# Slot ids loaded one expert block earlier, narrow blocks turned two steps later, and second-norm statistics split between two engines

## The chip, the cores and the metric

One Trainium2 chip, of which the kernel uses one core. The metric is the device time of one execution in microseconds (us); every kernel is run several times and the median is quoted. The engines of the core are PE (TensorE, matrix products), ACT (ScalarE), DVE (VectorE), POOL (GpSimd) and SP (SyncE, which here only issues transfers). Each takes its instructions in program order, and transfers (DMAs) run beside them.

## The reference, cut to what matters

The model is one layer: a token mixer (two recurrent head groups), a first layer norm, a mixture of 32 experts, a second layer norm. There are 2048 tokens of width 1024, all in float32. The change touches the last two parts.

```python
# experts: every token goes to 2 of 32 experts
hid = jax.nn.silu(xb @ w1[e]) * (xb @ w3[e])      # 1024 -> 512
y = hid @ w2[e]                                   # 512 -> 1024
f[tok] += weight * y
# second norm
r = ALPHA * h + g2 * f
mu, var = mean(r), mean((r - mu) ** 2)
out = (r - mu) * rsqrt(var + 1e-6) * ln2_g + ln2_b
```

## The kernel before, in words

Before the experts, each token's normed row is written to a DRAM tensor `u2D`, `ALPHA * h` to a DRAM accumulator `accD`, and a table `idxD` in DRAM receives, for each expert, the token number and the weight of each of its rows ("slot ids": 8 bytes a row). The experts are ranked by their load, and `ROWS` says how many rows are computed for the expert of each rank (288 down to 80). What exceeds it is left to a loop over further blocks of 128 rows at the end.

**Blocks.** The expert stage is a list of 33 blocks, unrolled. Block 0 is 128 rows of the largest expert. From block 1 on, wide blocks (odd numbers up to 27; 288-128 = 160, 224, 176, 160 or 144 rows, class `Wide`) and narrow blocks (even numbers; 80 to 128 rows, class `Block`) alternate; blocks 28 to 32 are all narrow, of 128 rows. For a block, the rows are gathered from `u2D` by an indirect DMA on POOL's queue into a tile `X` (three buffers; a wide block takes two), which needs the block's ids in a small tile `ix` (loaded by SP from `idxD`). PE transposes `X` four chunks at a time (L1330, "turn"), and ACT and DVE split the transposed chunk into a high and a low part (L1334, L1335) since the products are made of three reduced-precision products each. Then come four steps (`up(0)` to `up(3)`) of products with w1 and w3, the gate (`hidden`), a transpose of the gated rows for a narrow block (`turn_hidden`), and the products with w2 (`down`, L1341 to L1343). `put` weights the result on DVE (L1350) and adds it into `accD` by an indirect DMA on POOL's queue (L1351).

**Weights.** An expert has 12 pieces of 512 KB. SP fetches them into eight `raw` buffers (L1307); ACT casts the high part (L1314), DVE subtracts for the low part (L1315). `pump` does the next split that buffers allow, and SP's next fetch stands right behind it in SP's queue.

**Order.** Everything is written out by the loop over blocks `t` and steps `s_`. At step 0 of block t, `prepare(t + 2)` loads the ids of block t+2 on SP and issues its gather on POOL at once. A wide block t+1 is turned in all four steps of block t. A narrow block t+1 is turned in its steps 0 and 2. The downs of a narrow block t-1 are emitted in step 1 of block t, those of a wide block in its own step 3 and the next block's step 3.

**Second norm.** At the end, `accD` is read back as 16 tiles `f` of 128 tokens. Four functions, one tile apart, run over them: `stats2` (mean and variance: two `bn_stats` and one `bn_aggr` on DVE), `scale2` (`rstd_of`: an add of epsilon on DVE, L901, and a power on POOL, L902), `norm2` (the bias -mean*rstd as a one-column DVE instruction, L1665, and the normalization on ACT, L1666), and `affine2` (times the gain on DVE, L1669, where the gain lies in PSUM; plus the bias on POOL, L1673, or on DVE for the tiles in `DADD`, L1671; then the store). `ASTAT` lists tiles whose statistics would be taken by two passes on ACT; before, it is empty.

Of the kernel before, what the change touches and what calls it, by code (L numbers as in the profile page):

```python
# [10 lines left out]
I32 = mybir.dt.int32  # L11
# [3 lines left out]
ALU = mybir.AluOpType  # L15
# [12 lines left out]
ALPHA = 2.0 ** 0.25  # L28
EPS = 1e-6
FAR = -3.0e38  # L30
ASTAT = ()
DADD = (13, 14, 15)
LAG = 1

ROWS = [288] + [224] * 4 + [176] * 3 + [160] * 2 + [144] * 4 + [128] * 6 + [112] * 2 + [96] + [80] * 9
# [39 lines left out]
def hymba_kernel(ctx, tc, xT, ctxT, x, small, rows, ada_w, w_in, gate_w, w_out, router_w, w1, w3, w2, out):  # L75
    nc = tc.nc
    dve, act, pe, pool, sp = nc.vector, nc.scalar, nc.tensor, nc.gpsimd, nc.sync
# [604 lines left out]
    slots = []  # L682
# [62 lines left out]
    for si in range(len(slots), 3, -1):  # L745
        a, b, c, d = slots[si - 4:si]
        turn = si == len(slots) or slots[si][0] != d[0] or (si - 4 > 0 and slots[si - 5][0] != a[0])
# [157 lines left out]
    with ExitStack() as st:  # L905
# [239 lines left out]

        def turn_lead(X):
            pts = []
# [140 lines left out]
    with ExitStack() as st:  # L1288
# [5 lines left out]
        ex = st.enter_context(tc.tile_pool(name="ex", bufs=2))  # L1294
# [21 lines left out]
            k = 4 if n < 8 else 2  # L1316
            return [t.rearrange("p (k c) -> p k c", k=k) for t in (hi, lo)]

        def gather(row, n):

            ix = ex.tile([128, 2], I32, name="ix", tag="ix", bufs=8)
            sp.dma_start(ix[:n], idxD[bass.ds(row, n), :])
            X = ex.tile([128, D], F32, name="X", tag="X", bufs=3)
            pool.indirect_dma_start(out=X[:n], out_offset=None, in_=u2D, in_offset=bass.IndirectOffsetOnAxis(ap=ix[:n, 0:1], axis=0))  # L1324
            return ix, X

        def turned(X, n, k0):
            pt = psT.tile([128, 4, 128], F32, name="ptx", tag="pt")
            for k in range(4):
                pe.transpose(pt[:, k, :n], X[:n, 128 * (k0 + k):128 * (k0 + k) + 128], ident[:n, :n])  # L1330
            return pt[:, :, :n]

        def split_rows(xh, xl, pt):
            act.copy(xh, pt)  # L1334
            dve.tensor_sub(xl, pt, xh.bitcast(F32))  # L1335
# [9 lines left out]
        def put(py, ix, n):  # L1345

            y = ex.tile([128, D], F32, name="y", tag="y")
            for nh in range(2):
                s = slice(512 * nh, 512 * nh + 512)
                dve.scalar_tensor_tensor(y[:n, s], py[nh][:n], ix[:n, 1:2].bitcast(F32), g2[:n, s], op0=ALU.mult, op1=ALU.mult)  # L1350
            pool.indirect_dma_start(out=accD, out_offset=bass.IndirectOffsetOnAxis(ap=ix[:n, 0:1], axis=0), in_=y[:n], in_offset=None, compute_op=ALU.add)  # L1351
# [4 lines left out]
        class Block:  # L1356
# [3 lines left out]
            def __init__(self, row, n, weights, slot):  # L1360
                self.row, self.n, self.w, self.slot = row, n, weights, slot

            def gather(self):
                self.ix, self.X = gather(self.row, self.n)

            def places(self):
                x = ex.tile([128, KC, 2, 128], F32R, name="xx", tag=self.slot, bufs=1)
# [11 lines left out]
            def turn(self, i):  # L1379
                if i == 0:  # L1380
                    self.places()
                k0 = 4 * i
                split_rows(self.xh[:, k0:k0 + 4, :], self.xl[:, k0:k0 + 4, :], turned(self.X, self.n, k0))
# [37 lines left out]
        class Wide:  # L1421
# [5 lines left out]
            def __init__(self, row, n, weights, slot):  # L1427
                self.row, self.n, self.m, self.w, self.slot = row, n, n // 2, weights, slot

            def gather(self):  # L1430
                self.src = [gather(self.row + self.m * a, self.m) for a in range(2)]

            def turn(self, i):
                n, m = self.n, self.m
                if i == 0:
                    self.x = ex.tile([128, KC, 2, n], F32R, name="xw", tag=self.slot, bufs=1)
                a, k0 = i // 2, 4 * (i % 2)
                s = slice(m * a, m * a + m)
                split_rows(self.x[:, k0:k0 + 4, 0, s], self.x[:, k0:k0 + 4, 1, s], turned(self.src[a][1], m, k0))

            def up(self, s, kk):

# [29 lines left out]
                down(self.hh[:, k, s], self.hl[:, k, s], self.w[8 + k], k, self.py, self.m)  # L1472

            def put(self, part):
                put(self.py, self.src[part][0], self.m)

        SP = (mybir.EngineType.SP,)
        SPP = (mybir.EngineType.SP, mybir.EngineType.Pool)
# [17 lines left out]
        nb = len(blocks)  # L1496
        wide = [n > 128 for _, _, n, _ in blocks] + [False]

        def reg(s_):
            if s_ not in regs:  # L1500
                regs[s_] = nc.values_load(etab[0:1, sched[s_]:sched[s_] + 1], engines=SP, min_val=0, max_val=31)
            return regs[s_]
# [27 lines left out]
        if True:  # L1530
            B = []
            rest = overflow()

            def prepare(t):
                if t < nb:
                    s_, o, n, _ = blocks[t]
                    slot = "xw" if wide[t] or (not wide[t - 1] and B[t - 1].slot == "xs") else "xs"
                    B.append((Wide if wide[t] else Block)(reg(s_) * LE + o, n, weights[s_], slot))
                    B[t].gather()

            def finish(t, part):
                for k in range(4):
                    while 8 + k not in B[t].w:
                        pump(1)
                    B[t].down(k, part)
                    if blocks[t][3] and part == B[t].parts - 1:
                        state["down"] += 1
                    pump(1)
                B[t].put(part)

            def turn(t, i):
                if t < nb and i < B[t].turns:
                    B[t].turn(i)

            def used(t, i):
                if blocks[t][3]:
                    state["up"] += 2

            def late(t):
                if t == nb // 2:  # L1560
                    sp.dma_start(l2b, rows[0:1, 4096 + 3 * D:4096 + 4 * D].to_broadcast([128, D]))


            fetch_to(2)
            B.append(Block(reg(0) * LE, 128, weights[0], "xs"))
            prepare(1)
            prepare(2)
            fetch_to(NRAW)
            B[0].lead(lead_ix, lead_pt)
            pump(4)  # L1570
            for t in range(nb):
                for s_ in range(4):
                    while 2 * s_ + 1 not in B[t].w:
                        pump(1)
                    if wide[t]:
                        for kk in range(4):
                            B[t].up(s_, kk)
                            if kk == 1:
                                pump(1)
                    else:  # L1580
                        B[t].up(s_)
                    used(t, s_)
                    if s_ % 2 and wide[t]:
                        B[t].hidden(s_ // 2)
                    if s_ == 3 and not wide[t]:
                        B[t].hidden()
                    if s_ == 0 and t and not wide[t - 1]:
                        B[t - 1].turn_hidden()
                    if t + 1 < nb and wide[t + 1]:
                        turn(t + 1, s_)  # L1590
                    elif s_ % 2 == 0:
                        turn(t + 1, s_ // 2)
                    pump(2)
                    if s_ == 0:
                        if t:
                            prepare(t + 2)
                        late(t)
                    if s_ == 2 and t:
                        next(rest, 0)
                    if s_ == 1 and t and not wide[t - 1]:  # L1600
                        finish(t - 1, 0)
                    if s_ == 3 and t and wide[t - 1]:
                        finish(t - 1, 1)
                    if s_ == 3 and wide[t]:
                        finish(t, 0)
            B[nb - 1].turn_hidden()
            finish(nb - 1, 0)
# [4 lines left out]
        with tc.For_i(0, nov) as i:  # L1612
            oe = ex.tile([1, 2], I32, name="oe", tag="oe")
            for k in range(2):
                sp.dma_start(oe[:, k:k + 1], otD[0:1, bass.ds(i + k * (NOV + 2), 1)])
            e = nc.values_load(oe[0:1, 0:1], engines=ENG, min_val=0, max_val=31)
            row = nc.values_load(oe[0:1, 1:2], engines=ENG, min_val=0, max_val=32 * LE - 128)
            b = Block(row, 128, {}, "xs")
            b.gather()
            b.turn(0)  # L1620
            b.turn(1)
            for n in range(12):
                b.w[n] = split(fetch(e, n), n)
            for s_ in range(4):
                b.up(s_)
            b.hidden()
            b.turn_hidden()
            for k in range(4):
                b.down(k)
            b.put()  # L1630


    with ExitStack() as st:
# [12 lines left out]
        mv, rs = {}, {}  # L1646

        def stats2(i):

            mv[i] = gs.tile([128, 2], F32, name="mv2")  # L1650
            if i in ASTAT:
                sq = gp.tile([128, D], F32, name="sq2", bufs=1)
# [9 lines left out]
            rs[i] = rstd_of(gs, mv[i][:, 1:2], 1, 1.0 / D if i in ASTAT else 1.0)  # L1662

        def norm2(i):
            dve.scalar_tensor_tensor(mv[i][:, 0:1], mv[i][:, 0:1], 1.0 if i in ASTAT else -1.0, rs[i], op0=ALU.mult, op1=ALU.mult)  # L1665
            act.activation(f[i], f[i], AF.Identity, scale=rs[i], bias=mv[i][:, 0:1])  # L1666

        def affine2(i):
# [60 lines left out]
```

## Time and profile before

| | |
|---|---|
| median of 3 runs | 2242.07 us (2241.68 to 2252.21) |
| profiled execution, its own time | 2243.1 us |
| its span, first to last instruction | 2241.0 us |
| mean granted clock of PE in it | 0.957 |
| first `up` of the experts, last `put` | 1353.8 us, 2167.1 us |
| second norm, first `bn_stats` to the last instruction | 2178.0 us to 2237.4 us |

Times in the profile count from the first instruction of the span. A row of the timeline says when an instruction or a merged run of them started, how long it took, and in brackets how long its engine had stood idle and for what. "xN" is the number of instructions merged.

### The profile page before, as it was taken

To read this page: it belongs to the slowest core of one execution; us is meant where nothing else is said; L and a number is where in the kernel's file an instruction comes from. 1 tells how busy PE (TensorE), PEld (TensorE's weight loads), DVE (VectorE), ACT (ScalarE), POOL (GpSimd) and SP (SyncE) were. 2 spreads that over 40 slices of the span, in tenths; PEclk is the share of its full clock that TensorE was granted. 3 is DMA by queue.
4 is the path that set the end of the run, shared out by engine and by line. 5 is a ranking of instruction groups with operands and counts; after the bars stand their busy time and mean duration, and the time that the engine had idled before them with its cause. 6 is when DMAs were issued, how large, how long until landed. Compare 5 with 4: busy or idle time off the path is not lost. (4 is left out here: it accounts for less than half of the span.)

```text
span 2241.0 us, 34527 instructions
## 1 busy us (share of the span) xinstructions
PE 2048.3 (91%) x12440; PEld 1810.6 (81%) x12440; DVE 1713.6 (76%) x2632; ACT 1167.9 (52%) x1863; POOL 700.3 (31%) x532
## 2 busy tenths in 40 slices
PE   7999998999998999989799987999999999999960
PEld 3788778999997988889588877888888888788850
DVE  6677776866866888888677875788877788787869
ACT  3456554644655545535444324566665666565633
POOL 5121142222333232231466661112222223222116
PEclk9999999999999999999899987999999999999985
DMA  8324333323334144244765527899998989898965
GB/s 267 107 102 138 105 127 129 131 94 123 105 100 153 58 162 145 70 149 165 263 206 174 158 78 277 245 294 303 294 303 276 306 295 299 286 310 301 334 215 237
DMA packets 180515, 441.56 MB, mean 197 GB/s; under 512 B 27365, under 2 KB 69349, under 8 KB 179830
## 3 DMA queue, kind: packets, MB, share of 16 engines
q1 hardware_dynamic: 155446, 385.18, 49.6%
q0 software_dynamic: 15088, 46.81, 8.5%
q10 hardware_dynamic: 9808, 7.34, 1.0%
q8 instruction: 99, 1.62, 0.3%
q14 instruction: 74, 0.61, 0.1%
HBM read 358.63 MB, written 80.63 MB: 196 GB/s over the span
## 5 line engine op out<-in xcount | busy, mean ns | idle before, releaser
L1315 DVE TENSOR_TENSOR wlo<-raw,whi 128x1024 fp32r<-128x1024 f32 x384 | 452.3, 1220 | 55.4 <-ACT whi L1314 51.0
L356 PE MATMUL pp<-uh,wh 128*128 128x384 f32 (+2 forms) x1248 | 445.5, 357 | 4.6 <-ACT uh L246 2.3
L357 PE MATMUL pp<-ul,wh 128*128 128x384 f32 (+2 forms) x1248 | 429.1, 344 | 4.8 <-DVE ul L247 4.6
L358 PE MATMUL pp<-uh,wl 128*128 128x384 f32 (+2 forms) x1248 | 427.6, 343 | 3.0 <-DVE wl L247 3.0
L1314 ACT CAST whi<-raw 128x1024 fp32r<-128x1024 f32 x384 | 382.5, 1050 | 38.8 <-PE pye L1342 23.1
L1452 PE MATMUL ph<-xw,whi 128*128 128x448 f32 (+3 forms) x896 | 259.6, 365 | 1.6 <-DVE hid L1403 1.6
L356 PEld LDWEIGHTS pp<-uh,wh 128*128 128x128 f32 x1248 | 238.5, 191 | 26.3 <-ACT rgs L614 5.9
L357 PEld LDWEIGHTS pp<-ul,wh 128*128 128x128 f32 x1248 | 238.4, 191 | 19.8 <-DVE ul L247 10.3
L358 PEld LDWEIGHTS pp<-uh,wl 128*128 128x128 f32 x1248 | 237.5, 190 | 13.4 <-DVE wl L247 4.6
L1453 PE MATMUL ph<-xw,wlo 128*128 128x224 f32 (+3 forms) x896 | 222.3, 248 | 0.0
L388 POOL TENSOR_SCALAR mraw<-mraw,sil 128x512 f32<-128x512 f32 x56 | 99.7, 1780 | 363.1 <-DMA mraw<-in_ada_w_dram 363.1
L1351 POOL DMA_INDIRECT accD<-y,ix x46 | 113.1, 2459 | 316.5 <-DVE y L1350 315.9
L1452 PEld LDWEIGHTS ph<-xw,whi 128*128 128x128 f32 x896 | 174.7, 195 | 7.2 <-DVE hid L1403 1.8
L1395 PE MATMUL ph<-whi,xx 128*80 128x256 f32 (+3 forms) x608 | 175.3, 288 | 3.7 <-ACT whi L1314 3.5
L1453 PEld LDWEIGHTS ph<-xw,wlo 128*128 128x128 f32 x896 | 177.2, 198 | 1.2
L1397 PE MATMUL ph<-wlo,xx 128*80 128x256 f32 (+3 forms) x608 | 172.2, 283 | 1.4 <-DVE wlo L1315 1.4
L1396 PE MATMUL ph<-whi,xx 128*80 128x256 f32 (+3 forms) x608 | 171.6, 282 | 0.0
L1324 POOL DMA_INDIRECT X<-u2D,ix x46 | 65.5, 1425 | 320.8 <-PE pye L1343 134.3
L489 PE MATMUL pa<-Q,km 128*128 128x128 f32 x896 | 124.0, 288 | 19.2 <-DVE Q L492 11.9
L489 PEld LDWEIGHTS pa<-Q,km 128*128 128x128 f32 x896 | 118.4, 193 | 25.1 <-ACT K L419 7.0
L247 DVE TENSOR_TENSOR wl<-wr,wh 128x1024 fp32r<-128x1024 f32 x84 | 109.7, 1306 | 34.8 <-ACT wh L246 34.7
L490 DVE COPY_PREDICATED A<-masks,pa 128x384 f32<-128x384 uint8 (+1 forms) x140 | 84.1, 618 | 46.9 <-PE pa L489 44.1
(350 smaller groups left out, 4566.7 us busy)
## 6 DMA issues: line engine op xcount, KB each, us to landing
raw<-in_w_dram SPq DMA_DIRECT2D x384, 512.0 KB
wr<-in_w_in_dram SPq DMA_DIRECT2D x84, 512.0 KB
mraw<-in_ada_w_dram SPq DMA_DIRECT2D x64, 256.0 KB
aw<-in_ada_w_dram SPq DMA_DIRECT2D x16, 512.0 KB
fx<-in_x_dram SPq DMA_DIRECT2D x16, 512.0 KB
accD<-fr SPq DMA_DIRECT2D x16, 512.0 KB
u2D<-fu SPq DMA_DIRECT2D x16, 512.0 KB
f<-accD SPq DMA_DIRECT2D x16, 512.0 KB
```

Source lines behind the costliest of these rows:

```text
L356: pe.matmul(ps, wh[:, k, :], uh[:, k, :], start=k == 0, stop=False)
L357: pe.matmul(ps, wh[:, k, :], ul[:, k, :], start=False, stop=False)
L358: pe.matmul(ps, wl[:, k, :], uh[:, k, :], start=False, stop=k == KC - 1)
L489: pe.matmul(pa[:, c, :], km[:, s:s + 128], cut(Q, s, [(2 * b, 64 // b), (T + b, 2), (1, b)]), start=True, stop=True)
L1314: act.copy(hi, raw)
L1315: dve.tensor_sub(lo, raw, hi.bitcast(F32))
L1351: pool.indirect_dma_start(out=accD, out_offset=bass.IndirectOffsetOnAxis(ap=ix[:n, 0:1], axis=0), in_=y[:n], in_offset=None, compute_op=AL ...
L1395: pe.matmul(p, self.xh[:, k, :], wh[:, kk, :], start=k + g == 0, stop=False, skip_group_check=True)
L1396: pe.matmul(p, self.xl[:, k, :], wh[:, kk, :], start=False, stop=False, skip_group_check=True)
L1397: pe.matmul(p, self.xh[:, k, :], wl[:, kk, :], start=False, stop=k == KC - 1, skip_group_check=True)
L1452: pe.matmul(p[:, :2 * n], wh[:, kk, f], self.x[:, k].rearrange("p h t -> p (h t)"), start=k == 0, stop=False)
L1453: pe.matmul(p[:, :n], wl[:, kk, f], self.x[:, k, 0, :], start=False, stop=k == KC - 1)
```

## The change

Three things change. First, the load of a block's ids (`slots`) is separated from its gather. At step 0 of block t the kernel now gathers block t+2, whose ids were loaded during block t-1, and loads the ids of block t+3; the id tile has nine buffers instead of eight. Second, a narrow block t+1 is turned in steps 2 and 3 of block t instead of 0 and 2. Third, in the second norm the tiles 1, 3, 5, 7, 9, 11 and 13 take their statistics on ACT (a pass `Identity` with scale -1/1024 and a sum, then a pass `Square` with that sum as bias, summed again), the bias is added on DVE for tiles 3, 7, 11 and 15 instead of 13, 14 and 15, and the one-column instruction of `norm2` becomes a `tensor_scalar` whose operand `rs` is a per-partition scalar, where it was a `scalar_tensor_tensor` with `rs` as a second tensor.

```diff
-ASTAT = ()
-DADD = (13, 14, 15)
+ASTAT = (1, 3, 5, 7, 9, 11, 13)
+DADD = (3, 7, 11, 15)
...
-        def gather(row, n):
-
-            ix = ex.tile([128, 2], I32, name="ix", tag="ix", bufs=8)
+        def slots_of(row, n):
+
+            ix = ex.tile([128, 2], I32, name="ix", tag="ix", bufs=9)
             sp.dma_start(ix[:n], idxD[bass.ds(row, n), :])
+            return ix
+
+        def gather(ix, n):
+
             X = ex.tile([128, D], F32, name="X", tag="X", bufs=3)
             pool.indirect_dma_start(out=X[:n], out_offset=None, in_=u2D, in_offset=bass.IndirectOffsetOnAxis(ap=ix[:n, 0:1], axis=0))
-            return ix, X
+            return X
...
             def prepare(t):
+
                 if t < nb:
+                    B[t].gather()
+                place(t + 1)
+
+            def place(t):
+                if len(B) <= t < nb:
                     s_, o, n, _ = blocks[t]
                     slot = "xw" if wide[t] or (not wide[t - 1] and B[t - 1].slot == "xs") else "xs"
                     B.append((Wide if wide[t] else Block)(reg(s_) * LE + o, n, weights[s_], slot))
-                    B[t].gather()
+                    B[t].slots()
...
             B.append(Block(reg(0) * LE, 128, weights[0], "xs"))
+            place(1)
+            place(2)
             prepare(1)
             prepare(2)
             fetch_to(NRAW)
...
                     if t + 1 < nb and wide[t + 1]:
                         turn(t + 1, s_)
-                    elif s_ % 2 == 0:
-                        turn(t + 1, s_ // 2)
+                    elif s_ >= 2:
+                        turn(t + 1, s_ - 2)
...
         def norm2(i):
-            dve.scalar_tensor_tensor(mv[i][:, 0:1], mv[i][:, 0:1], 1.0 if i in ASTAT else -1.0, rs[i], op0=ALU.mult, op1=ALU.mult)
+            dve.tensor_scalar(mv[i][:, 0:1], mv[i][:, 0:1], rs[i], 1.0 if i in ASTAT else -1.0, op0=ALU.mult, op1=ALU.mult)
             act.activation(f[i], f[i], AF.Identity, scale=rs[i], bias=mv[i][:, 0:1])
```

## Rows read from the trace of the kernel before

**Rows 1.** Busy time of engines by stretch: start:end, length, engines, clock, DMA share, GB/s.

```profile
1500.00:1600.00 100.00, 99.54 (x643) 87.04 (x642) 80.06 (x93) 62.39 (x80) 22.54 (x13) 1.00 0.91 296
...
2180.00:2241.00 61.00, 0.00 (x0) 0.00 (x0) 56.25 (x96) 19.85 (x16) 39.70 (x29) 0.50 0.62 251
```

**Rows 2.** Waits, 1390 to 2165 us: us in total, times, longest.

```profile
PE ptx L1330 <- DMA X<-u2D,ix: 19.3, 9, 4.4
```

**Rows 3.** Timeline of PE: transposes at step 0 of wide blocks 13, 25, 27, 29.

```profile
1684.20 0.44 PE L1330 MATMUL ptx<-ident,hid 80*128 80x80 f32 x4
...
1985.72 0.55 PE L1330 MATMUL ptx<-ident,hid 112*128 112x112 f32 x4
...
2032.66 0.60 PE L1330 MATMUL ptx<-ident,hid 128*128 128x128 f32 x4
2037.69 1.09 PE L1330 MATMUL ptx<-ident,X 128*128 128x128 f32 x4 [4.42 <-DMA X<-u2D,ix]
...
2084.71 0.60 PE L1330 MATMUL ptx<-ident,hid 128*128 128x128 f32 x4
```

**Rows 4.** Busy time by stretch, right behind a wait of PE.

```profile
1690.00:1700.00 10.00, 10.00 (x48) 8.21 (x48) 6.61 (x9) 5.74 (x9) 2.12 (x2) 0.81 0.65 183
```

**Rows 5.** Timeline of POOL and of SP's queue in block 12.

```profile
1667.28 3.87 POOL L1351 DMA_INDIRECT accD<-y,ix  x1 [11.34 <-DVE y L1350]
1671.40 0.34 SPq L1322 DMA_DIRECT2D ix<-idxD  x1
1679.88 1.69 POOL L1324 DMA_INDIRECT X<-u2D,ix  x1 [8.74 <-PE pye L1342]
```

**Rows 6.** Busy time by stretch: two blocks without a wait; a late narrow block.

```profile
1985.70:2032.70 47.00, 46.44 (x327) 40.39 (x327) 39.23 (x47) 30.25 (x40) 13.65 (x6) 1.00 0.94 313
...
2096.30:2116.30 20.00, 18.89 (x138) 17.72 (x137) 18.27 (x20) 13.83 (x16) 2.77 (x3) 1.00 1.03 383
```

**Rows 7.** Timeline at the start of the experts: SP's queue, ACT.

```profile
1354.23 2.03 SPq L1322 DMA_DIRECT2D ix<-idxD  x3
...
1360.21 1.04 ACT L1314 CAST whi<-raw 128x1024 fp32r<-128x1024 f32 x1 [5.25 <-DMA raw<-in_w_dram]
```

**Rows 8.** Timeline of the second norm, one period of it.

```profile
2189.29 2.34 POOL L1673 TENSOR_TENSOR f<-f,l2b 128x1024 f32<-128x1024 f32 x1 [0.72 <-DVE f L1669]
...
2190.59 1.06 DVE L1665 SCALAR_TENSOR_TENSOR mv<-mv,rstd 128x1 f32<-128x1 f32 x1
2191.57 1.21 DVE L1669 TENSOR_TENSOR f<-f,l2g 128x1024 f32<-128x1024 f32 x1
2191.59 0.55 POOL L902 TENSOR_TENSOR rstd<-rstd,nhalf 128x1 f32<-128x1 f32 x1
...
2192.70 1.27 DVE L1658 BATCH_NORM_STATS2 bs<-f 128x6 f32<-128x512 f32 x2
```

**Rows 9.** Timeline of the second norm: its first gain product, and its end.

```profile
2184.43 1.22 DVE L1669 TENSOR_TENSOR f<-f,l2g 128x1024 f32<-128x1024 f32 x1
...
2228.64 1.22 DVE L1669 TENSOR_TENSOR f<-f,l2g 128x1024 f32<-128x1024 f32 x1
2229.89 2.08 DVE L1671 TENSOR_TENSOR f<-f,l2b 128x1024 f32<-128x1024 f32 x1
2230.85 1.53 POOL L902 TENSOR_TENSOR rstd<-rstd,nhalf 128x1 f32<-128x1 f32 x1
...
2236.13 1.23 DVE L1671 TENSOR_TENSOR f<-f,l2b 128x1024 f32<-128x1024 f32 x1
```

**Rows 10.** Timeline of the first norm: DVE beside a POOL product.

```profile
1207.89 3.45 POOL L1029 TENSOR_TENSOR fr<-fr,l1g 128x1024 f32<-128x1024 f32 x1 [3.83 <-DVE fu L1027]
...
1209.42 0.21 DVE L1101 TENSOR_SCALAR tok<-tok,c 128x1 f32<-128x1 f32 x1
```

**Rows 11.** Instructions of ACT by line: duration ns min/median/max.

```profile
L969 ACT ACTIVATION_READ_ACCUMULATOR sq<-fo x64: 185/187/190, 1076.4 to 1291.7; 128x1 f32 x64
...
L1666 ACT ACTIVATE f<-f,mv,rstd x16: 1239/1241/1242, 2183.0 to 2232.6; 128x1024 f32<-128x1024 f32 x16
```

More of the change, by code (lines that the diff above doesn't have):

```diff
@@ L1361, in __init__, with slots @@
                 self.row, self.n, self.w, self.slot = row, n, weights, slot
+            def slots(self):
+                self.ix = slots_of(self.row, self.n)
             def gather(self):
-                self.ix, self.X = gather(self.row, self.n)
+                self.X = gather(self.ix, self.n)
             def places(self):
@@ L1428, in __init__, with slots @@
                 self.row, self.n, self.m, self.w, self.slot = row, n, n // 2, weights, slot
+            def slots(self):
+                self.ix = [slots_of(self.row + self.m * a, self.m) for a in range(2)]
             def gather(self):
-                self.src = [gather(self.row + self.m * a, self.m) for a in range(2)]
+                self.X = [gather(ix, self.m) for ix in self.ix]
             def turn(self, i):
@@ L1438, in turn @@
                 s = slice(m * a, m * a + m)
-                split_rows(self.x[:, k0:k0 + 4, 0, s], self.x[:, k0:k0 + 4, 1, s], turned(self.src[a][1], m, k0))
+                split_rows(self.x[:, k0:k0 + 4, 0, s], self.x[:, k0:k0 + 4, 1, s], turned(self.X[a], m, k0))
             def up(self, s, kk):
@@ L1474, in put @@
             def put(self, part):
-                put(self.py, self.src[part][0], self.m)
+                put(self.py, self.ix[part], self.m)
         SP = (mybir.EngineType.SP,)
@@ L1618, in hymba_kernel @@
             b = Block(row, 128, {}, "xs")
+            b.slots()
             b.gather()
```

## The prediction, made before any run of the change

> **What bounds the kernel now.** I read the busy times by stretch first. In the expert stage PE is the bound: 99.5 us of 100 at full clock in its first half, with DVE at 80, ACT at 62 and the DMA engines at a share of 0.91 [rows 1]. In the second norm PE does nothing and DVE is busy 56 of 61 us. The rest of the kernel, up to 1340 us, isn't touched by the diff. So two questions decide: where does PE stand still among the experts, and what paces the second norm?
>
> The waits answer the first. PE stands 19.3 us in nine waits, all of them transposes of gathered rows that have not landed [rows 2]. I then looked up each on PE's timeline: none lies before 1684 us; seven, together 16.9 us, stand at step 0 of wide blocks 13 to 27, where the rows of the next, narrow block are turned, and the last two, 2.5 us, in the closing run of narrow blocks. The reader should see one of them in [rows 3]: the gated rows are transposed at 2032.66, the next four transposes only at 2037.69.
>
> A wait costs more than its length. Just behind one, PE is busy for 10 us of 10 but was granted a clock of 0.81, part of the time 1.2 instead of 2.4 GHz [rows 4]. So I priced the waits by whole periods instead. From block 13 to block 29 there are eight pairs of a wide and a narrow block, 2084.71 - 1684.20 = 400.5 us; the pair without a wait takes 2032.66 - 1985.72 = 46.9 us [rows 3]. Eight pairs at 47 are 376 us: the waits with their clock cost 24 us.
>
> POOL's timeline and SP's queue tell why the rows are late [rows 5]. In block 12 POOL is through with its previous scatter at 1667.28 + 3.87 = 1671.15. SP issues the id load for block 14 only at 1671.40, because it stands behind weight fetches that wait for buffers. The gather starts at 1679.88, after 8.74 us idle. (The profile puts that idle time down to a product of PE; that is an inference from semaphores, and the id load in flight explains it.) PE asks for these rows right after 1684.20 + 0.44 and gets them at 1687.5, so issue to landing is 7.6 us.
>
> **The expert stage, part by part.** With ids a block early nothing holds the gather but the scatter ahead of it on POOL: it goes at about 1671.3 instead of 1679.9 and lands at about 1679, before step 0 needs it. The turn moves as well: a wide block takes about 27 us (a pair's 47 less the 20.0 of a narrow block [rows 6]), steps 0 and 1 about half of that, so rows are asked for near 1696. The margin is some 17 us; all seven waits should go. I take -24 us (bounds: -16.9, the waits alone, if the clock stays; -24.5).
>
> The last two waits, 2.5 us, lie where PE isn't alone: in a late narrow block DVE is busy 18.3 of 20.0 us and the DMA share is 1.03 at 383 GB/s, against 0.94 at 313 GB/s in the clean pair [rows 6]. With the transfers full, weights will take over part of the wait. Between 0 and -2.5 I take -1.
>
> What the moved steps cost: the splits of a turn (on ACT and DVE) now come one or two steps before the product that reads them instead of three or four. Behind a wide block 24 downs stand between, so this is 0. Among the four last narrow blocks the cover is one `up`, under 3 us, and DVE is nearly full; bounds 0 to +4, I take 0, since ACT has 6 us in 20 idle there [rows 6]. The 46 id loads and 46 gathers stay as many. The ninth id buffer keeps SP free: block t+3's ids overwrite those of block t-3, whose last scatter is issued at the end of block t-2, with a whole wide block, 27 us, between.
>
> At the start the new order loads ids of blocks 1, 2 and 3 instead of 1 and 2 before the third weight piece: five SP loads instead of three, which took 2.03 us, or 0.68 each [rows 7]. ACT stands 5.25 us for that piece, so nothing covers it: +1.4 us (bounds 0 and +1.4).
>
> **The second norm, part by part.** Its period is 3.57 us a tile, (2191.57 - 2184.43) / 2 [rows 8, 9]. The rows show a ring, and DVE's work isn't what fills it: POOL's bias add ends at 2191.63; the one-column DVE instruction, which needs only the power finished long before, runs from 2190.59 to 2191.65 and ends with that add, then the gain product follows (1.13 us to the next instruction), and only then POOL's next add. So a two-tensor DVE instruction in SBUF stands until POOL is through. The bias add on DVE does the same (2.08 us at 2229.89 against 1.23 at 2236.13), and POOL's power behind it stands too (1.53 against 0.55); a gain product with its second operand in PSUM runs 1.22 at 2228.64 regardless.
>
> Does the new `tensor_scalar` also stand? In the first norm such an instruction, one column with a pointer scalar, took 0.21 us in the midst of a POOL product from 1207.89 to 1211.34 [rows 10]. So I price it at 0.21 (bounds 0.21 and the 1.06 of the old one), and the ring is cut. What then paces is the busiest engine over four tiles (two with ACT statistics, one DVE add, three POOL adds):
> - the SBUF path that POOL and two-tensor DVE instructions take in turn: 3 x 2.35 + 4 x 0.55 + 1.2 = 10.4 us;
> - ACT: four normalizations at 1.24, and two tiles with two more passes, each 1.24 + 0.19 for reading its sum [rows 11]: 5.0 + 5.7 = 10.7 us. Passes of this length with a sum aren't in the trace; the normalization row is the nearest;
> - DVE: two tiles of statistics at 1.27, four gain products at 1.13, the add at 1.2 and a dozen one-column instructions at 0.21 or less: under 10.8 us.
>
> All three lie close, 10.7 against 14.3 before: 2.68 a tile. From the first gain product, sixteen tiles take 42.8 us and the last bias add 1.2, 44 us, where before it was 2236.13 + 1.23 - 2184.43 = 52.9 [rows 9]. Queues that take turns in order lose a little of such a sum, about 1 us: -8 us (bounds -3 and -11).
>
> The Trainium skill speaks against this step. "SBUF — State Buffer", section "Who interferes with whom", says that VectorE and GpSimd share one port pair as an exclusive lock, that a two-input SBUF instruction takes part in it, and that `tensor_scalar` can too when it enters a two-port mode. By that the one-column instruction might stand as before; the row of 0.21 us says it doesn't, and the measurement decides.
>
> **The sum**, against the profiled execution's own 2243.1 us: -24 - 1 + 1.4 - 8 = -31.6, so 2211.5. The median of the runs stands 1.0 below that execution: 2210.
>
> **The rivals.**
> - *The transfers take back half.* DMA is busy 0.94 in the clean pair, and 1.03 is what a full stretch shows [rows 6]; PE's waits were also time for weights to catch up (a share of 0.65 behind one [rows 4]). Against it: the clean pair ran its 46.9 us at 0.94. If half the 24 comes back as waits for weights: 2222. Chance 0.12.
> - *The one-column instruction still stands* behind POOL. Then the ring stays; only the statistics move, which weren't its limit, and only the end changes: about -3 instead of -8, so 2215. Chance 0.08, for the skill's rule and because the exact operands aren't in the trace.
> - *The rows still come late*, because POOL's scatter, not the ids, holds the gather. Then only the second norm gains and the start loses: 2235.5. Against it stand 8.74 us of idle POOL. Chance 0.04.
> - *Slower: ids held too long.* If SP stood at an id load for its buffer, the weight fetches behind it would stand as well. Eight raw buffers at one piece per 2 us (a pair's 24 pieces in 47 us) cover 16 us, and the buffer is free 27 us before, so the scatter would have to release it some 43 us later than I think before PE notices; from there each of 30 blocks pays. At 1.5 us a block more, it eats the gain of 32 and 13 beyond: 2255. Chance 0.02.
> - *More than forecast*: the waits' clock is worth more and the second norm reaches its -11: 2204. Chance 0.06.
>
> The forecast itself has 0.68. The range 2199 to 2225 holds it and all but the third and fourth rivals. A difference of 0.5%, 11 us, is about what a measurement of this kernel can tell from none. Faster by more: 0.94; within: 0.04; slower: 0.02.
>
> **What would show it.** Right: no wait of PE for `X`; POOL's gathers directly behind scatters; granted clock 1.00 from 1400 us to the end of the experts; pairs of 47 us up to block 28; weights at the start 1.4 us later; in the second norm one-column instructions of 0.2 us, a period near 2.7 and ACT the busiest. Wrong: PE waiting for casts of weights with the DMA share at 1.03, one-column instructions of 1 us, or id loads waiting for scatters on SP.

## The result, and the profile after

| | before | after |
|---|---|---|
| median of the runs, us | 2247.14 (4 runs, 2241.68 to 2253.80) | 2209.06 (4 runs, 2205.26 to 2214.66) |
| profiled execution, us | 2243.1 | 2208.83 |
| its span, us | 2241.0 | 2206.8 |
| mean granted clock | 0.957 | 0.963 |

The ratio of the times on record is 0.985, with a 95% interval of 0.9819 to 0.9881: 1.2 to 1.8% faster. (The medians of the table alone divide to 0.983; the one of the kernel before was 2242.07 ahead of the forecast, and a fourth run, 2253.80, moved it.) The forecast was 2210, with a range of 2199 to 2225.

Because totals move by several microseconds from one execution to the next, I compare stages. The marks are the first `up` product of the experts, the transposes of `hid` at step 0 of a block, and the first statistics of the second norm; all are read from PE's and DVE's timelines.

| stage, us | before | after | difference |
|---|---|---|---|
| start to the first `up` (not touched) | 1353.8 | 1355.0 | +1.15 |
| first `up` to step 0 of block 1 | 31.09 | 31.65 | +0.56 |
| to block 13 | 299.28 | 299.25 | 0.0 |
| block 13 to block 29, eight pairs | 400.51 | 372.17 | -28.3 |
| block 29 to the last `hid` | 73.76 | 71.58 | -2.2 |
| to the first statistics of the second norm | 19.53 | 20.87 | +1.3 |
| to the end of the program | 63.0 | 56.3 | -6.7 |

They add up to -34.2, the difference of the spans; the forecast's sum was -31.6.

First, the waits of PE among the experts, new kernel (total us, times, longest), to set beside [rows 2]:

```profile
PE ptx L1334 <- DVE hid L1410: 1.4, 1, 1.4
PE ph L1462 <- DVE hid L1410: 1.3, 1, 1.3
PE pye L1345 <- ACT hw L1338: 1.0, 1, 1.0
```

These are the three largest that are left from 1380 us on. No wait for `X` is among the rest either: 19.3 us in nine waits are gone. What that is worth shows in PE's busy time and clock over the whole stretch of the eight pairs, before and then after:

```profile
1684.20:2084.71 400.51, 381.52 (x2579) 331.26 (x2578) 313.69 (x366) 240.80 (x317) 101.16 (x47) 0.97 0.90 295
```

```profile
1685.88:2058.05 372.17, 370.87 (x2579) 322.53 (x2577) 312.30 (x365) 239.48 (x317) 105.05 (x47) 1.00 0.98 317
```

The columns are those of [rows 1]. PE's idle time fell from 19.0 to 1.3 us, which gives 17.7 of the 28.3 us, and its busy time by 10.65, while the granted clock rose from 0.97 to 1.00. Next, POOL and SP's queue in block 12, to set beside [rows 5], and PE's timeline in blocks 13 and 29, to set beside [rows 3]:

```profile
1668.97 3.87 POOL L1355 DMA_INDIRECT accD<-y,ix  x1 [13.96 <-DVE y L1354]
1672.57 0.93 SPq L1322 DMA_DIRECT2D ix<-idxD  x2
1673.15 0.95 POOL L1328 DMA_INDIRECT X<-u2D,ix  x1 [0.31 <-PE ptx L1334]
```

```profile
1685.88 0.44 PE L1334 MATMUL ptx<-ident,hid 80*128 80x80 f32 x4
...
1700.30 0.44 PE L1334 MATMUL ptx<-ident,X 80*128 80x80 f32 x4
...
2058.05 0.60 PE L1334 MATMUL ptx<-ident,hid 128*128 128x128 f32 x4
```

The gather starts 0.31 us behind the scatter instead of 8.74 us, and every gather from 1644 to 2060 us starts 0.30 or 0.31 us behind POOL's instruction ahead of it. The ids that SP loads just then are those of a later block. PE turns the gathered rows at 1700.30, 14.4 us after step 0 begins and 27 us after the gather was issued. Between the first and the last mark lie the eight pairs: 372.17 us, 46.5 each.

The busy time by stretch, in the columns of [rows 1], shows the transfers' side: the middle of the pairs, a late narrow block, and 4 us among the last downs.

```profile
1830.00:1880.00 50.00, 49.94 (x347) 42.99 (x347) 42.52 (x52) 31.90 (x44) 15.34 (x8) 1.00 0.98 310
2097.00:2117.00 20.00, 20.00 (x147) 18.91 (x147) 19.86 (x21) 15.78 (x19) 1.56 (x1) 1.00 1.03 376
2130.00:2134.00 4.00, 3.32 (x10) 2.16 (x9) 0.69 (x1) 0.58 (x1) 0.00 (x0) 0.60 0.56 109
```

PE is busy 49.94 of 50 us at full clock with the DMA share at 0.98; PE's list has no wait for weights there. In the late narrow block PE now has 20.0 of 20.0 us and DVE 19.86 ([rows 6] had 18.89 and 18.27). The last row belongs to the +1.3 us that the forecast didn't have: a granted clock of 0.60 while the last downs run, so 1.2 GHz for most of these 4 us. The kernel before had 1.00 at this place.

The start, to set beside [rows 7]: the first `up` of PE, SP's id loads, PE's first transposes of block 1's rows, ACT's cast of the third weight piece.

```profile
1354.98 0.55 PE L1402 MATMUL ph<-whi,xx 128*128 128x256 f32 x1 [3.43 <-ACT whi L1314]
...
1355.39 3.68 SPq L1322 DMA_DIRECT2D ix<-idxD  x5
...
1362.36 0.79 PE L1334 MATMUL ptx<-ident,X 80*128 80x80 f32 x4 [0.51 <-DMA X<-u2D,ix]
...
1364.05 1.04 ACT L1314 CAST whi<-raw 128x1024 fp32r<-128x1024 f32 x1 [7.94 <-DMA raw<-in_w_dram]
```

Five loads take 3.68 us on the queue, and the third piece is cast 9.07 us behind the first `up`, where before it was 6.38 (1360.21 - 1353.83). In the same stretch the kernel before had a wait for rows that [rows 2], which begins at 1390 us, doesn't count:

```profile
1363.31 0.80 PE L1330 MATMUL ptx<-ident,X 80*128 80x80 f32 x4 [3.20 <-DMA X<-u2D,ix]
```

It is 0.51 us in the new kernel.

Last, one stretch of the second norm, to set beside [rows 8], and the one-column line over all sixteen tiles (duration in ns: min/median/max):

```profile
2172.50 2.36 POOL L1692 TENSOR_TENSOR f<-f,l2b 128x1024 f32<-128x1024 f32 x1
2172.57 0.21 DVE L1684 TENSOR_SCALAR mv<-mv,rstd 128x1 f32<-128x1 f32 x1 [0.20 <-POOL rstd L902]
2172.70 1.21 DVE L1688 TENSOR_TENSOR f<-f,l2g 128x1024 f32<-128x1024 f32 x1
...
2175.34 2.35 POOL L1692 TENSOR_TENSOR f<-f,l2b 128x1024 f32<-128x1024 f32 x1
...
2177.19 1.60 DVE L1690 TENSOR_TENSOR f<-f,l2b 128x1024 f32<-128x1024 f32 x1
```

```profile
L1684 DVE TENSOR_SCALAR mv<-mv,rstd x16: 202/212/216, 2155.3 to 2195.4; 128x1 f32<-128x1 f32 x16
```

POOL's add runs from 2172.50 to 2174.86, and in its first tenth of a microsecond the one-column instruction starts and takes 0.21 us. The old one took 1.06 and ended with the add. The gain product then takes 1.21 us under the same add (its second operand is in PSUM), and POOL's next add follows after 2.84 us instead of a period of 3.57. In the middle of the new kernel's second norm the gain products of four tiles take 10.97 us, so 2.74 a tile. The bias add on DVE still pays: 1.60 us here, 1.2 when alone. The engines' busy time from the first gain product to the end of the last add, in the columns of [rows 1]:

```profile
2156.79:2201.12 44.33, 0.00 (x0) 0.00 (x0) 39.31 (x68) 31.41 (x39) 37.66 (x25) 0.50 0.70 283
```

### The profile page after: what moved, and what is told of

Read it like the earlier page. It is cut to its first block, busy times and chain, and to the rows that moved or that the text cites. A ratio compares the mean times of both kernels' runs of the same rounds, so it can differ in the third digit from the quotient of the medians.

```text
span 2206.8 us, 34512 instructions
## 1 busy us (share of the span) xinstructions
PE 2039.6 (92%) x12440; PEld 1802.6 (82%) x12440; DVE 1694.3 (77%) x2612; ACT 1182.6 (54%) x1891; POOL 703.1 (32%) x531
## 3 DMA queue, kind: packets, MB, share of 16 engines
q1 hardware_dynamic: 155446, 385.18, 50.7%
## 5 line engine op out<-in xcount | busy, mean ns | idle before, releaser
L1462 PE MATMUL ph<-xw,whi 128*128 128x448 f32 (+3 forms) x896 | 249.8, 354 | 1.3 <-DVE hid L1410 1.3
L1462 PEld LDWEIGHTS ph<-xw,whi 128*128 128x128 f32 x896 | 168.3, 188 | 6.9 <-DVE hid L1410 1.5
L1463 PEld LDWEIGHTS ph<-xw,wlo 128*128 128x128 f32 x896 | 171.1, 191 | 1.2
L1001 PE MATMUL py<-woh,mh 128*128 128x512 f32 x256 | 113.8, 445 | 1.9 <-ACT mh L985 1.9
```

The source lines that it names most:

```text
L1462: pe.matmul(p[:, :2 * n], wh[:, kk, f], self.x[:, k].rearrange("p h t -> p (h t)"), start=k == 0, stop=False)
L1463: pe.matmul(p[:, :n], wl[:, kk, f], self.x[:, k, 0, :], start=False, stop=k == KC - 1)
```

## The experiments

Times of one kernel vary by some microseconds, and the first `up` alone came between 1353.8 and 1359.6 us, in a part that no kernel here touches. So the verdicts below go by stage, with the total beside it. On the chip of the first four kernels the kernel before took 2249.96 us in one run.

**Early ids alone.** The new kernel, with the turns and the second norm's split of before; its one-column instruction is left as the new `tensor_scalar`.

```
-ASTAT = (1, 3, 5, 7, 9, 11, 13)
-DADD = (3, 7, 11, 15)
+ASTAT = ()
+DADD = (13, 14, 15)
...
-                    elif s_ >= 2:
-                        turn(t + 1, s_ - 2)
+                    elif s_ % 2 == 0:
+                        turn(t + 1, s_ // 2)
```

> Two edits that meet nowhere, each read in its own stage. Experts: the new kernel with its early slot ids, but narrow blocks turned in steps 0 and 2 as before. Theory: the id load was what made the gather late; alone it brings the rows about 5 us ahead of step 0, so PE waits for X under 1 us in all, and the eight pairs from block 13 to block 29 take 376 us (before 400.5, new kernel 372.2). Rival (the scatter on POOL holds the gather, and only the later turn helped): waits for X of 10 us or more remain and the pairs take over 388. Second norm: statistics and adds on the engines of before, only the one-column instruction new. Theory: that instruction alone cuts the ring; from the first bn_stats to the end of the last bias add 51 us (before 59.4, new kernel 50.6). Rival (the split of the statistics is what shortened it): 56 or more.

Measured: 2213.13 us in one run; the pairs 373.97 us; the second norm 54.4 to the end of the program, and its last add ends 50.7 us after the first statistics, against 50.6 in the new kernel. Behind block 0 no wait for `X` is left.

**The later turn alone**, with the new split of the second norm but the old one-column instruction: the kernel before with

```
-ASTAT = ()
-DADD = (13, 14, 15)
+ASTAT = (1, 3, 5, 7, 9, 11, 13)
+DADD = (3, 7, 11, 15)
...
-                    elif s_ % 2 == 0:
-                        turn(t + 1, s_ // 2)
+                    elif s_ >= 2:
+                        turn(t + 1, s_ - 2)
```

> Experts: the kernel before, with ids loaded and rows gathered as it did, only the narrow blocks turned in steps 2 and 3. Theory: rows land as late as before (7 to 8 us behind the gather) but are asked for some 12 us later, so the waits for X are gone here too and the eight pairs take 372 to 376 us; if the later turn also fills PE's short wait for the gated rows at step 3, they lie at the lower end, below the run with early ids alone. Rival (ids must be early): waits of 10 us or more remain, over 388. Second norm: statistics and adds as in the new kernel, with the old one-column instruction. Theory: the ring stays, 57 us (before 59.4). Rival (the statistics split does it): 52 or less.

Measured: 2211.59 us in one run; the pairs 370.53 us; the second norm 62.4. Here too no wait for `X` is left behind block 0, though the gathers are as late as ever: POOL still stands idle for 4.3 to 10.2 us ahead of each one for a narrow block. So each half takes away all nine waits by itself, and the later turn is 3.4 us better. Part of that is a second, small wait that it fills, PE's for the gated rows (total us, times, longest), in the trace of early ids alone:

```profile
PE pye L1345 <- ACT hw L1338: 1.7, 4, 0.5
```

It stands with 1.5 us in four waits before, and it isn't in the list of the kernel with the later turn. The second norm of that kernel shows the ring still whole:

```profile
2174.10 2.34 POOL L1673 TENSOR_TENSOR f<-f,l2b 128x1024 f32<-128x1024 f32 x1
2174.17 2.29 DVE L1665 SCALAR_TENSOR_TENSOR mv<-mv,rstd 128x1 f32<-128x1 f32 x1
...
2176.39 1.21 DVE L1669 TENSOR_TENSOR f<-f,l2g 128x1024 f32<-128x1024 f32 x1
```

```profile
L1665 DVE SCALAR_TENSOR_TENSOR mv<-mv,rstd x16: 142/156/2292, 2152.4 to 2197.0; 128x1 f32<-128x1 f32 x16
```

Its first statistics and its last add:

```profile
2147.24 1.29 DVE L1658 BATCH_NORM_STATS2 bs<-f 128x6 f32<-128x512 f32 x2 [11.08 <-DMA f<-accD]
...
2201.82 2.07 DVE L1671 TENSOR_TENSOR f<-f,l2b 128x1024 f32<-128x1024 f32 x1
```

One column takes 0.15 us when POOL is idle and 2.29 us when its add has just begun; then it ends with that add and the gain product follows. From the first statistics to the end of the last add it is 56.7 us, against 59.4 before and 50.6 with the `tensor_scalar`. So the new split of statistics and adds alone gives 2.7 of the 8.8 us up to there (and 0.7 to the end of the program, for a reason that the next kernel shows); and since early ids alone had the `tensor_scalar` with the old split and took 50.7, this split gives nothing that shows on top of it.

**The start and the end put right.** The new kernel with block 3's ids behind the weight piece, and the last three bias adds on DVE:

```
-            prepare(1)
-            prepare(2)
-            fetch_to(NRAW)
+            B[1].gather()
+            B[2].gather()
+            fetch_to(NRAW)
+            place(3)
...
-DADD = (3, 7, 11, 15)
+DADD = (13, 14, 15)
```

> The new kernel with two edits. Start of the experts: block 3's ids loaded behind the eighth weight piece instead of ahead of the third. Theory: SP issues the third piece 1.4 to 1.7 us earlier, the cast that waits for it starts that much earlier against the first product of the experts (new kernel 9.07 us behind it, before 6.38), and the end of block 0 follows by 0.6 to 1.4 us. Rival (the piece is late for another reason, such as the transfers): no change beyond 0.3 us. Second norm: bias adds of tiles 13, 14 and 15 on DVE instead of 3, 7, 11 and 15. Theory: little, 50 to 52 us against 50.6, as the port that POOL and DVE share is loaded the same. Rival: without DVE's share in the middle POOL is the bound, 54 or more.

Measured: 2209.28 us in one run. The third piece is cast 6.49 us behind the first `up` (9.07 in the new kernel, 6.38 before), and step 0 of block 1 comes after 31.06 instead of 31.65, so the 2.6 us of the late piece are worth 0.6 here. A wait for rows takes the place of the one for weights: PE stands 3.99 us for the first rows of block 1, where the new kernel stood 0.51:

```profile
1369.75 0.80 PE L1334 MATMUL ptx<-ident,X 80*128 80x80 f32 x4 [3.99 <-DMA X<-u2D,ix]
```

The new kernel itself took 31.65 and 33.02 us in two executions, so 0.6 is within what this stage varies by. The second norm takes 54.7 us to the end of the program instead of 56.3, though its last add ends 0.4 later (51.0 against 50.6). What was saved lies behind the last add. The release of the engines at the end of the program (the line behind the last one of the kernel; durations in ns), new kernel and then kernel before:

```profile
L1744 POOLq DRAIN  x3: 46/115/9157, 2196.8 to 2206.6; - x3
L1744 SPq DRAIN  x3: 7/7/13, 2204.1 to 2206.2; - x3
```

```profile
L1725 POOLq DRAIN  x3: 46/115/9681, 2228.6 to 2240.8; - x3
L1725 SPq DRAIN  x3: 7/7/13, 2240.1 to 2240.5; - x3
```

In the new kernel POOL's long drain ends at 2196.8 + 9.16 = 2206.0, after SP's, which begins at 2204.1 when the last store is out; the program ends 0.8 us later. POOL's last add ended at 2200.04, so the drain runs 5.9 us on. Before, it ended at 2238.3, hidden behind SP's drain at 2240.1. The tail shows it in every kernel: from the end of the last add to the end of the program it is 3.7 us where the last two or three adds are on DVE (before, early ids alone, this one), and 5.7 us, in both kernels, with `DADD` (3, 7, 11, 15), where the end lies 6.8 us behind POOL's last add. The drain ends 5.9 us behind POOL's last instruction in all of them.

**Six raw buffers.** Was the reserve in the transfers as large as the forecast's first rival needed it not to be? The new kernel with

```
-NRAW = 8
+NRAW = 6
...
-ASTAT = (1, 3, 5, 7, 9, 11, 13)
-DADD = (3, 7, 11, 15)
+ASTAT = (1, 4, 7, 10, 13)
+DADD = (3, 6, 9, 12, 15)
```

> The new kernel with two edits. Experts: six raw weight buffers instead of eight, so transfers can run ahead of the splits by a quarter less. Theory: the transfers have slack once the waits are gone, so the eight pairs take 372 to 378 us and PE's waits for casts grow by under 3 us. Rival (the transfers are nearly the bound, and were about to take back the gain): over 384 us, with waits for casts of weights in the narrow blocks. Second norm: statistics of tiles 1, 4, 7, 10, 13 on ACT and bias adds of tiles 3, 6, 9, 12, 15 on DVE. Theory: the three engines are balanced a little better, 49 us from the first bn_stats to the end of the last add. Rival: no better than the new kernel's 50.6.

Measured: 2234.15 us in one run, and the pairs take 389.0 us, 17 more. My theory fell: it held 378 at most. The waits of ACT from 1700 to 2050 us, then those of PE in the whole expert stage:

```profile
ACT whi L1314 <- DMA raw<-in_w_dram: 31.5, 33, 3.2
```

```profile
PE pye L1345 <- ACT hw L1338: 15.0, 9, 3.2
```

The new kernel has this wait of ACT once, for 1.3 us; with six buffers it has it 33 times. PE doesn't wait for weights by name: it stands 15.0 us for gated rows, because ACT's part of them is queued behind a cast that waits for its piece. A list of waits read for weights alone would have missed it. The second norm came out as expected: its last add ends 48.3 us after the first statistics, 2.3 less than in the new kernel. So a split does pay on top of the `tensor_scalar` where it is better balanced, with five tiles' statistics on ACT instead of seven and five adds on DVE instead of four.

**Two lines.** The kernel before with two edits only: the later turn, and the `tensor_scalar`.

```
-                    elif s_ % 2 == 0:
-                        turn(t + 1, s_ // 2)
+                    elif s_ >= 2:
+                        turn(t + 1, s_ - 2)
...
-            dve.scalar_tensor_tensor(mv[i][:, 0:1], mv[i][:, 0:1], 1.0 if i in ASTAT else -1.0, rs[i], op0=ALU.mult, op1=ALU.mult)
+            dve.tensor_scalar(mv[i][:, 0:1], mv[i][:, 0:1], rs[i], 1.0 if i in ASTAT else -1.0, op0=ALU.mult, op1=ALU.mult)
```

> The kernel before with two lines changed and nothing else: narrow blocks turned in steps 2 and 3, and the one-column instruction of the second norm. Ids, their buffers, statistics and bias adds stay as they were. Theory: these two lines hold the whole gain. Eight pairs 370 to 373 us without a wait for X, first bn_stats to the end of the program 54.4 us (before 63.0, new kernel 56.3), and the time is 2 to 6 us below the new kernel on this chip. Rival (the earlier ids or the split statistics each carry some microseconds of it): 3 us or more above the new kernel.

**Two lines and a balance.** The same, with

```
-ASTAT = ()
-DADD = (13, 14, 15)
+ASTAT = (1, 4, 7, 10, 13)
+DADD = (3, 6, 9, 12, 14, 15)
```

> The two lines, and in the second norm the statistics of tiles 1, 4, 7, 10 and 13 on ACT and the bias adds of tiles 3, 6, 9, 12, 14 and 15 on DVE, so that POOL's last instruction lies earlier. Theory: POOL's drain at the end of the program takes 5.9 us from its last instruction, and in the new kernel it, not the last store, ends the program; with the last two adds on DVE it is hidden again and the balance saves 1 us more: first bn_stats to the end of the program 53 us, 1 to 2 us below the run with the two lines alone, 4 to 7 us below the new kernel. Rival (the end is set by the last store alone, and its length varies): 55 us or more.

**The new kernel again**, on the same chip as these two:

> The new kernel itself, on the same chip as the two before it. Theory and rival alike: 0.98 to 0.988 of the kernel before; eight pairs 372 us, first bn_stats to the end of the program 56.3 us.

| kernel | median us | runs | ratio to before, 95% interval |
|---|---|---|---|
| two lines | 2205.05 | 5, 2199.55 to 2206.60 | 0.983 (0.9805 to 0.9856) |
| two lines and a balance | 2202.54 | 5, 2200.70 to 2203.08 | 0.9827 (0.9803 to 0.985) |
| new kernel again | 2210.83 | 6, 2209.71 to 2213.41 | 0.9867 (0.9845 to 0.9888) |
| before | 2242.55 | 11, 2234.09 to 2250.34 | |

The intervals of the ratios overlap, but of the runs on this chip no one of the first two kernels is as slow as the fastest of the new one: two lines do all of the change's work and end 5.8 us lower, with the balance 8.3 lower, more than the 4 to 7 expected. By stages of the profiled executions:

| stage, us | new kernel | new kernel again | two lines | two lines, balance |
|---|---|---|---|---|
| first `up` to block 1 | 31.65 | 33.02 | 30.12 | 29.01 |
| to block 13 | 299.25 | 299.1 | 297.91 | 297.84 |
| to block 29 | 372.17 | 371.28 | 370.72 | 370.96 |
| to the last `hid` | 71.58 | 71.3 | 70.9 | 70.9 |
| to the second norm | 20.87 | 19.29 | 21.07 | 19.48 |
| to the end | 56.3 | 56.3 | 54.2 | 52.1 |

Without the early ids each stage of the experts is a little shorter: 1.5 to 4 us at the start, 1.2 to 1.4 to block 13, 0.3 to 1.5 in the pairs, 0.4 to 0.7 behind them. In the stage to block 13, which has none of the long waits, four kernels make a table of two by two: 299.28 before, 300.66 with early ids alone, 297.86 with the later turn alone, 299.25 with both. The early ids cost 1.4 us there and the later turn brings 1.4. PE's busy time in this stage says what kind of cost it is, the two lines first and then the new kernel again (columns of [rows 1]):

```profile
1388.70:1686.61 297.91, 297.25 (x1965) 261.79 (x1964) 236.20 (x285) 178.07 (x232) 64.28 (x37) 1.00 0.90 288
```

```profile
1390.53:1689.63 299.10, 298.40 (x1964) 263.39 (x1963) 236.09 (x285) 177.72 (x232) 57.91 (x35) 1.00 0.91 286
```

Of 1.19 us, 1.15 are busy time at the same clock, for as many products but one: PE doesn't wait longer, its products take longer.

In the last stage the two lines are 2.1 us below the new kernel, nearly all of it by the tail, with their last adds on DVE. The balance brings 2.1 more, and not by the tail, which is 3.7 us in both: its last add ends 48.4 us after the first statistics, that of the two lines 50.5. Its last lines:

```profile
2190.36 2.35 POOL L1673 TENSOR_TENSOR f<-f,l2b 128x1024 f32<-128x1024 f32 x1 [0.64 <-DVE f L1669]
2190.46 1.22 DVE L1669 TENSOR_TENSOR f<-f,l2g 128x1024 f32<-128x1024 f32 x1
2191.72 2.08 DVE L1671 TENSOR_TENSOR f<-f,l2b 128x1024 f32<-128x1024 f32 x1
2193.72 1.21 DVE L1669 TENSOR_TENSOR f<-f,l2g 128x1024 f32<-128x1024 f32 x1
2194.96 1.22 DVE L1671 TENSOR_TENSOR f<-f,l2b 128x1024 f32<-128x1024 f32 x1
```

POOL is through at 2192.71 and DVE at 2196.18, so POOL's drain lies in the shade of the last two tiles. The add of 2.08 us that has to stand for POOL's is the one beside it; the next takes 1.22.

**Seven raw buffers, and all bias adds on POOL.** The two lines with

```
-NRAW = 8
+NRAW = 7
...
-DADD = (13, 14, 15)
+DADD = ()
```

> The two lines with two further edits. Experts: seven raw weight buffers instead of eight. Theory (from six, which cost 17 us over the eight pairs): the reserve is used up step by step, so seven cost 3 to 9 us, pairs 374 to 380. Rival (eight is exactly enough and each buffer below costs the same 8 to 9 us, or there is a reserve of one): 371 to 373, no cost at seven. Second norm: all sixteen bias adds on POOL. Theory of the drain: POOL ends last, some 51.5 us after the first bn_stats, and the program ends 6.7 us behind that, 58 us. Rival (the last store ends the program): it ends 3.7 us behind, 55 us.

Measured: 2207.02 us in one run; the pairs 370.52, as with eight buffers; 72.52 from block 29 to the last `hid`, 1.6 more; the second norm 58.4 to the end of the program. ACT's waits for pieces from 1700 to 2050 us, and POOL's sixteen adds:

```profile
ACT whi L1314 <- DMA raw<-in_w_dram: 13.7, 18, 1.8
```

```profile
L1673 POOL TENSOR_TENSOR f<-f,l2b x16: 2345/2352/2371, 2154.7 to 2196.1; 128x1024 f32<-128x1024 f32 x16
```

ACT stands 13.7 us for pieces, and none of it reaches PE in the pairs: one buffer can be spared (here without early ids), two can't (there with them). I had expected a step for each buffer, and that fell. On the other half, POOL's last add ends at 2198.5 and the program at 2205.3, 6.8 us later, as the drain theory had it. The sixteen adds themselves are 51.6 us behind the first statistics, only 1.1 us later than with three of them on DVE.

## Why the prediction was right

- **The seven waits** (-24 forecast, -28.3 measured). The mechanism was right: the id load held the gather, and its rows now land well before PE turns them. Its size was too small by 4 us. The forecast priced eight pairs at 47 us from the one pair without a wait, but the later turn makes every pair a little shorter than that one, 46.5 us on the mean; of this, 1.5 us are the waits for gated rows seen above, and the rest is spread too thin for the lists. Early ids alone took 373.97 us, 2 below the 376 worked out; the later turn alone took 370.53, and both together 372.17. What the forecast didn't see is that the two halves do the same work twice; it argued the whole gain from the ids and counted the later turn as margin. That the waits cost their clock as well was right: 10.6 of the 28.3 us are busy time, with the clock at 1.00 instead of 0.97.
- **The last two waits** (-1 forecast, -2.2 measured). The transfers took back less than expected, at a share of 1.03 in that stretch. The bound of -2.5 held.
- **The moved splits and the ninth id buffer** (0 forecast). No new wait of PE came of the splits. The early ids have a price all the same: from the first `up` to the last `hid`, 774.7 us with them, 772.4 with the start put right, 768.7 to 769.8 with the later turn alone. From step 0 of block 1 on, so without the start, they cost 1.7 to 3.5 us, where the forecast had none. No wait in the lists accounts for it. Its largest part lies in the products with w1 and w3 of the 80-row blocks, which follow each other every 117 or 118 ns (medians) in all five kernels with early ids and every 113 or 114 ns in all five without, 102.9 us against 100.3 or 100.4 over the stage. The ninth id buffer came with the early ids in each of these kernels, and no run separates the two, so the cause stays open.
- **The start** (+1.4 forecast, +0.6 measured, and +1.9 in the new kernel's other execution). The loads took 3.68 us instead of 2.03, 1.65 more where 1.4 was worked out, and the piece came 2.7 us later. The forecast held that nothing covers it. PE's wait for block 1's rows does in part: it was 3.20 us before and is 0.51 now. The forecast's reading that no wait lies before 1684 us had missed it, because its list began at 1390.
- **The one-column instruction** (0.21 forecast, 0.202 to 0.216 measured). This step decided the second norm. The old instruction stood for POOL's add (2.29 us beside one, 0.15 without), the new one never did in sixteen tiles. The Trainium skill's page "SBUF — State Buffer", section "Who interferes with whom", says that a VectorE instruction with two inputs in SBUF contends with a GpSimd instruction that reads SBUF, and that `tensor_scalar` can contend in a two-port mode. The first agrees with the 2.29 us; of the second the 0.21 us show nothing at this size.
- **The second norm** (-8 forecast, -6.7 measured). To the end of the last add it is 59.4 - 50.6 = 8.8 us, within 1 us of the term. Then 2.0 us go to the tail, because POOL's drain lies bare when POOL adds up to the last tiles. The forecast looked at the last add and not behind it. The pace came out near the one worked out, 2.74 us a tile for 2.68, but not for the reason given: the forecast had ACT as the busiest engine and its statistics as a condition of that pace. ACT is busy 31.4 of 44.3 us, DVE 39.3 and POOL 37.7, and with the statistics left on DVE, in early ids alone, the gain products follow each other every 2.70 us. So the closeness of that number is in part luck. That the new split is worth little while the ring stands the rival had right: 2.7 us to the end of the last add, 0.7 to the end of the program, for about 3.
- **Neither forecast nor part of the change**: +1.3 us at a lower clock in the last downs, and +1.15 before the first `up`. The clock can't be laid to the change: the new kernel took 20.87 us there in one execution and 19.29 in another, the two-line kernels 21.07 and 19.48.

Of the rivals, the transfers' was nearer than its 0.12 says: with two buffers fewer the transfers took 17 of the 28 us. That the one-column instruction stands, that the rows come late, and that id loads hold up SP fell by the durations and waits above: behind block 0 PE's list has neither rows nor weights, and the kernel is no slower. That the total came out at 2209 for 2210 owes something to terms that cancel: 5.5 us more from the experts' waits, against the tail, the clock and the first `up`.

## What to carry to other kernels

Where a change holds two remedies for one wait, run each alone: here either took away all nine waits, and the simpler one, turning the rows two steps later, was better and cost nothing that shows. A wait can be removed by asking later as well as by fetching earlier. In a ring of two engines look first at the smallest instruction that one holds up for the other, and for its form: one line changed from a two-tensor to a one-tensor instruction gave the whole gain of the norm up to its last add, and a split of the work between engines paid only where it was balanced. And follow the end of a program past its last instruction: what an engine does last decides how long it takes to let go.

## What was not expected of the hardware

- POOL's drain at the end of the program went on 5.9 us behind its last instruction in all ten traces, which put the program's end 6.8 us behind POOL's last add in the kernel that had all adds there, against 3.7 us behind the last add on DVE where DVE had the last two or three.
- The DMA engines ran at shares of 0.97 to 0.99 and 310 to 339 GB/s in four stretches of 50 us of the pairs, and PE stayed busy 49.94 us and more of each; seven buffers of 512 KB were enough for the pairs and six were not, 0 us for the first buffer taken away (without early ids) and 17 for both (with them).
- PE's granted clock fell to 0.60 in a stretch of 4 us among the last downs, and the stage was 1.6 us shorter in another execution of the same kernel. What brings this on wasn't tried.
